# Head of a trunk kernel: the first key rows on ScalarE's DMA queue, the norm's sums four steps sooner, and three groups of edges that fix what follows what

## Chip, core and metric

The kernel runs on one core of one Trainium2 chip. The metric is the device time of one execution in microseconds (us). The kernel before takes 1174.61 us, the median of three runs (1174.42 to 1174.98). Profiles come from the hardware profiler, one execution each; times in a trace count from the start of its span.

## What is computed

One layer of a decoder trunk for 256 tokens of width 2048, in float32. The parts that this case touches:

```python
h = rms_norm(x, attn_norm[i])
z = h @ w_in[0]                                 # 2048 x 4384
zs = token_shift(z[..., POOL_WIDTH:], mu_shift) # z + (z_prev - z) * mu
...
w = -softplus(-(w0 + tanh(zw) @ w_up)) - 0.5
a = sigmoid(a0 + za @ a_up)
g = sigmoid(zg) @ g_up
```

z's columns are cut into a pool part, receptance (zr), key (zk), value (zv), each 1024 wide, and 288 columns of low-rank gates: 64 for zw, 64 for za, 160 for zg. Behind this come the pooling mixer, the RWKV scan with its norm, the output product, the feed-forward part with squared ReLU, a gated embedding and a last norm. All that is left as it is.

## The kernel before

Each weight panel (256 rows of the product, 512 columns, held as 128 partitions x 1024) is loaded as raw and split into a high part wh (ScalarE, two ACTIVATE of 512 columns, L168) and a low part wl (VectorE, one subtraction, L169). A product of tokens with such a panel is eight matmuls with wh (the activations' high part hTh at L244, low part hTl at L245) and then four with wl (L241), 512 columns each. raw, wh and wl have three buffers each, and a panel's load waits for the low part of the panel three before it.

The normed input is not made first: x is used with the norm's weight alone, and the factor 1/rms of each token (rs1) is put on the products as they leave the accumulators. So the squares' sums are needed only when the first product is copied out.

The head (L405 and on) runs two products side by side on the tensor engine (TensorE, PE in the profile): the 288 gate columns (wag_prod, in tiles of one or two rows of 128, banks wag_b) and the first key half (zk0, banks zk_b), whose generator gives its matmuls in steps. A step of a panel's first half is two matmuls, one of its second half a single one; a panel has eight steps. steps(n) gives n of them. ready(8) issues eight matmuls of ones ahead of the first operands. squares(q) squares a quarter of x on ScalarE and folds it on VectorE into the tile sqx; four matmuls with one column of ones then sum sqx over the partitions into sbank (L444). head_norm takes the root and the reciprocal. wag_out copies the gate banks out with rs1 as the scale (wagS), transposes them on TensorE (wagT, L467 and L468), and makes zf from them by shift_evac (an ACTIVATE, L338, and a VectorE operation that adds the token before, L339), with tanh on the first part and sigmoid on the rest. Behind that, z_zk0 finishes the key product, copies it out (zk0s, L491) and transposes it (zkT, L501).

What sets the order: TensorE's program order is the order of the code. VectorE's and ScalarE's is the code's only until early.close(), which stands behind wag_out. Calls under tc.high_priority are put forward by the scheduler, and tc.issue_after(ins) keeps an instruction of the same engine behind ins. The table behind does this for the ScalarE splits: behind["zk0_7"] = ins holds the split of panel 7 of zk0 (the eighth) behind ins. All loads of the head go through SP's queue in program order, except the parameters par_sb (ScalarE's queue, L83). GpSimd (POOL) makes constants early, then X (L715) and the four bands wband (L130 to L132), which VectorE finishes (L133 to L135); X lies in the memory of sqx's tiles and so waits for the matmuls that read them.

Of the kernel before, what the change touches and what calls it, by code (L numbers as in the profile page):

```python
# [16 lines left out]
T = 256  # L17
D = 2048
# [22 lines left out]
def trunk(  # L41
# [104 lines left out]

    deep = []

    def load_raw(src, n, name):
        own = False  # L150
        if deep:
            deep.append(name)
            own = len(deep) > 5 and len(deep) % 6 < 3
        if own:
            raw = fp.tile([128, 1024], F32, tag="raw2", bufs=3, name=f"raw_{name}")
        else:
            raw = wp.tile([128, 1024], F32, tag="raw", name=f"raw_{name}")
        nc.sync.dma_start(raw[:, 0:n], src)
        return raw

    def split_w(raw, name, after=None):

        wh = wp.tile([128, 1024], F32R, tag="wh", name=f"wh_{name}")
        wl = wp.tile([128, 1024], F32R, tag="wl", name=f"wl_{name}")
        with tc.high_priority(20000):
            for a in range(2):
                with tc.issue_after(after.ins) if after is not None else ExitStack():
                    nc.scalar.activation(wh[:, a * 512 : (a + 1) * 512], raw[:, a * 512 : (a + 1) * 512], AF.Copy)  # L168
            nc.vector.tensor_tensor(wl, raw, wh.bitcast(F32), op=ALU.subtract)  # L169
# [49 lines left out]

    behind = {}  # L220

    def gemm_toks(src, acts, name, consume, kps=None, hooks=()):

        banks = [mm_bank(f"{name}_b{i}") for i in range(2)]
        kps = list(range(src.shape[0])) if kps is None else kps
        hooks = dict(hooks)
        for i, kp in enumerate(kps):
            if kp in hooks:
                hooks[kp]()
            raw = load_raw(src[kp].rearrange("p a n -> p (a n)"), 1024, f"{name}_{kp}")  # L230
            halves = split_w(raw, f"{name}_{kp}", behind.get(f"{name}_{kp}"))
            for part in range(2):
                for a in range(2):
                    k = kp * 2 + a
                    a_ = acts(k)
                    ah, al = a_ if isinstance(a_, tuple) else (a_[:, 0, :], a_[:, 1, :])
                    for tt in range(2):
                        ts_ = slice(tt * 128, (tt + 1) * 128)
                        if part:
                            last = i == len(kps) - 1 and a == 1  # L240
                            nc.tensor.matmul(banks[tt], ah[:, ts_], halves[a][1], start=False, stop=last)  # L241
                            yield 0.23
                        else:
                            nc.tensor.matmul(banks[tt], ah[:, ts_], halves[a][0], start=i + a == 0, stop=False)  # L244
                            nc.tensor.matmul(banks[tt], al[:, ts_], halves[a][0], start=False, stop=False)  # L245
                            yield 0.45
        consume(banks)
# [105 lines left out]
    def load_xT(k0, n):  # L353
        nc.sync.dma_start(xq[k0 // 8][:, k0 // 4 % 2, k0 % 4 : k0 % 4 + n], xT[:, k0 : k0 + n, :])
# [46 lines left out]
    def ready(n):  # L401
        for _ in range(n):
            nc.tensor.matmul(rbank[:, 0:128], ones, ones, start=True, stop=True)

    def head():  # L405
        load_xT(0, 1)
        load_wag("tE", 0, 1)
        load_xT(1, 1)
        load_wag("tF", 1, 1)
        ready(8)  # L410
        wag_prod(0, 1)
        wag_prod(1, 1)
        steps(8)
        load_xT(2, 2)
        load_wag("zr", 2, 2)
        load_xT(4, 4)
        load_wag("zv", 4, 2)
        wag_prod(2, 2)
        wag_prod(4, 2)
        steps(8)  # L420
        sums.append(squares(0))
        load_wag("BK", 6, 2)
        load_xT(8, 4)
        load_wag("BKt", 8, 2)
# [12 lines left out]
        wag_prod(14, 2)
        steps(10)
        sums.append(squares(3))
        steps(3)  # L440
        derived()
        for tt in range(2):
            for i, q in enumerate((1, 3)):
                nc.tensor.matmul(  # L444
                    sbank[:, tt : tt + 1], sums[q][:, 0, tt * 128 : (tt + 1) * 128], ones[:, 0:1],
                    start=i == 0 and tt == 0, stop=i == 1, skip_group_check=True,
                )
        steps(1)

    rs1 = const.tile([128, 2], F32, tag="rs", bufs=2, name="rs_n1")  # L450

    def head_norm():
        nc.scalar.activation(rs1, sbank[:, 0:2], AF.Sqrt, bias=eps_n, scale=1.0 / D)
        nc.vector.reciprocal(rs1, rs1)

    zf = mixc.tile([128, 3, T], F32, name="zf")
    zwa, zg, zg2 = zf[:, 0], zf[:, 1], zf[0:64, 2]

    def wag_out():
        wagS = rp.tile([128, 576], F32, tag="SC", bufs=2, name="wagS")  # L460
        for tt in range(2):
            nc.scalar.activation(wagS[:, tt * 288 : (tt + 1) * 288], wag_banks[tt][:, 0:288], AF.Copy, scale=rs1[:, tt : tt + 1])
        tb, tb2 = rw_bank("wagT"), rw_bank("wagT2")
        for tt in range(2):
            c0 = tt * 288
            for i in range(2):
                nc.tensor.transpose(tb[:, i * T + tt * 128 : i * T + (tt + 1) * 128], wagS[:, c0 + i * 128 : c0 + (i + 1) * 128], ident)  # L467
            nc.tensor.transpose(tb2[0:32, tt * 128 : (tt + 1) * 128], wagS[:, c0 + 256 : c0 + 288], ident)  # L468
        mw = PARAM_COLS["mu_wag"]
        for i, (nm, src, pn) in enumerate((("zwa", tb[:, 0:T], 128), ("zg", tb[:, T : 2 * T], 128), ("zg2", tb2[0:32, 0:T], 32))):  # L470
            dst = zf[0:pn, i, :]
            shift_evac(dst, src, col("mu_wag", i)[0:pn], omu[0:pn, mw - m0 + i : mw - m0 + i + 1])
            if i == 0:
                nc.scalar.activation(dst[0:64], dst[0:64], AF.Tanh)
            else:
                nc.scalar.activation(dst, dst, AF.Sigmoid)
        nc.scalar.activation(zf[32:64, 2, :], zf[0:32, 2, :], AF.Copy)


    def z_product(i, tag, mu_name, gi, stage="a0"):  # L480

        box = []

        def consume(banks):
            if stage == "a0":
                zt = a8(0, f"{tag}{gi}s")[:, 0:1024].rearrange("p (a n) -> p a n", a=2)
            else:
                zt = rp.tile([128, 2, 512], F32, tag=stage, name=f"{tag}{gi}s")
            with tc.high_priority(30000):
                for tt in range(2):  # L490
                    nc.scalar.activation(zt[:, tt], banks[tt], AF.Copy, scale=rs1[:, tt : tt + 1])  # L491
            box.append(zt)

        def turn():
            zt = box.pop()
            dst = e4(tag)
            banks = [rw_bank(f"{tag}T{i}") for i in range(2)]
            for p in range(4):
                for tt in range(2):
                    o = p % 2 * T + tt * 128  # L500
                    nc.tensor.transpose(banks[p // 2][:, o : o + 128], zt[:, tt, p * 128 : (p + 1) * 128], ident)  # L501
            for p in range(4):
                c = PARAM_COLS[mu_name] - m0 + 4 * gi + p
                with tc.high_priority(30000):
                    shift_evac(dst[:, p, :], banks[p // 2][:, p % 2 * T : (p % 2 + 1) * T], col(mu_name, 4 * gi + p), omu[:, c : c + 1])
            return dst

        gen = queued(gemm_toks(w_in[i + gi], hT, f"{tag}{gi}", consume))

        def finished(us=1.70):  # L510
            finish(gen)
            fill(us)
            return turn()

        return finished
# [1052 lines left out]
```

## Time and profile before

| | |
|---|---|
| median of three runs | 1174.61 us |
| the profiled execution | 1175.37 us |
| its span | 1173.40 us |
| busy: TensorE, VectorE, ScalarE, GpSimd | 1160.2, 877.7, 713.5, 57.1 us |
| TensorE's clock as granted, mean | 0.999 |

The span is what the profiler saw of the core; the execution's time has 1.97 us more around it. In a timeline a row holds a run of like instructions: start, length of the run, engine, line, operation, output and inputs, shape, count, and in brackets the engine's idle time before with what ended it. Matmuls overlap, so the time of one in a stream is the distance of two starts, not its length.

### The profile page before, as it was taken

How to read it: one execution, taken by the hardware profiler on the slowest of the kernel's cores; microseconds unless marked ns; L12 is line 12 of the kernel's file. 1: busy time of each engine (PE TensorE's matmuls, PEld its weight loads, DVE VectorE, ACT ScalarE, POOL GpSimd, SP SyncE). 2: the span in 40 equal slices, each digit the busy share in tenths (PEclk: the TensorE clock that was granted, in tenths of full speed). 3: DMA queues.
4: the chain of work that ended last, by engine and by line, in shares of the span. 5: the costliest groups of instructions: out<-in, count | busy, mean ns of one | idle time of the engine just before them, and what ended most of it. 6: DMA issues, size and time to landing. Idle time of an engine off the chain costs nothing.

```text
span 1173.4 us, 17398 instructions
## 1 busy us (share of the span) xinstructions
PE 1160.2 (99%) x6407; PEld 972.1 (83%) x6407; DVE 877.7 (75%) x1194; ACT 713.5 (61%) x1323; POOL 57.1 (5%) x133
## 2 busy tenths in 40 slices
PE   9999999999999999999999999999999999999997
PEld 8788777888888888888888888888888888888886
DVE  7686996964756666766998997676768988897543
ACT  8776849676544565555664664555556665677543
POOL 2100000000000000000110110000000110000000
PEclk9999999999999999999999999999999999999999
DMA  7454343354455555565786786555555886975511
GB/s 292 154 202 147 131 139 117 129 180 161 161 200 178 180 183 194 197 216 180 223 246 213 229 254 218 193 186 193 184 193 165 260 254 220 323 241 188 197 55 72
DMA packets 67253, 224.42 MB, mean 191 GB/s; under 512 B 7712, under 2 KB 8480, under 8 KB 66784
## 3 DMA queue, kind: packets, MB, share of 16 engines
q1 hardware_dynamic: 60240, 207.38, 51.5%
q0 software_dynamic: 6496, 15.21, 5.7%
q8 instruction: 50, 0.82, 0.3%
q10 hardware_dynamic: 432, 0.73, 0.2%
q14 instruction: 35, 0.29, 0.1%
HBM read 221.19 MB, written 2.10 MB: 190 GB/s over the span
## 4 chain that ended last, share of the span: by engine, by line
PE 96%; DVE 2%; DMA 1%; ACT 1%; issue 0%; POOL 0%; SPq 0%; DVEq 0%; POOLq 0%; ACTq 0%
PE u_w L1136 20%; PE u_w L1141 10%; PE d_b L1293 7%; PE d_b L1295 7%; PE d_b L1294 7%; PE d_w L1293 2%; PE d_w L1295 2%; PE d_w L1294 2%; PE gt_b L244 2%; PE gt_b L245 2%; PE gt_b L241 2%; PE zp_b L241 1%; PE zv_b L244 1%; PE zv_b L241 1%; PE zk_b L244 1%; PE zv_b L245 1%
## 5 line engine op out<-in xcount | busy, mean ns | idle before, releaser
L1136 PE MATMUL u_w<-h,wh_u 128*128 128x512 f32 x1024 | 321.8, 396 | 0.0
L168 ACT ACTIVATE wh_u<-raw_u 128x512 fp32r<-128x512 f32 x256 | 147.5, 624 | 162.8 <-issue 101.8
L169 DVE TENSOR_TENSOR wl_u<-raw_u,wh_u 128x1024 fp32r<-128x1024 f32 x128 | 156.7, 1224 | 104.8 <-ACT wh_u L168 103.3
L1141 PEld LDWEIGHTS u_w<-h,wl_u 128*128 128x128 f32 x1024 | 192.7, 188 | 45.1
L1141 PE MATMUL u_w<-h,wl_u 128*128 128x256 f32 x1024 | 201.2, 278 | 0.0
L1136 PEld LDWEIGHTS u_w<-h,wh_u 128*128 128x128 f32 x1024 | 156.1, 189 | 0.2
L169 DVE TENSOR_TENSOR wl_gt<-raw_gt,wh_gt 128x1024 fp32r<-128x1024 f32 x24 | 29.4, 1224 | 23.2 <-ACT wh_gt L168 23.1
L173 ACT ACTIVATE wad<-ring 128x512 fp32r<-128x512 f32 x29 | 18.2, 628 | 43.9 <-DVE ring L1344 43.9
L168 ACT ACTIVATE wh_gt<-raw_gt 128x512 fp32r<-128x512 f32 x48 | 27.9, 633 | 24.2 <-PE gt_b L245 17.0
L244 PE MATMUL gt_b<-wh_gt,h 128*128 128x512 f32 x96 | 37.4, 390 | 0.0
L245 PE MATMUL gt_b<-wh_gt,h 128*128 128x512 f32 x96 | 37.4, 390 | 0.0
L1346 DVE TENSOR_TENSOR raw_d<-raw_d,ring 128x1024 f32<-128x1024 f32 x29 | 35.5, 1223 | 0.7
L1263 POOL DMA_DIRECT2D ring<-in_w_ffn_down_dram x29 | 16.5, 568 | 362.0 <-DVE wad L174 361.3
L1264 POOL DMA_DIRECT2D ring<-in_w_ffn_down_dram x29 | 25.3, 874 | 105.5 <-DMA ring<-in_w_ffn_down_dram 105.5
L169 DVE TENSOR_TENSOR wl_o<-raw_o,wh_o 128x1024 fp32r<-128x1024 f32 x16 | 19.6, 1223 | 12.9 <-ACT wh_o L168 11.4
L168 ACT ACTIVATE wh_o<-raw_o 128x512 fp32r<-128x512 f32 x32 | 18.4, 623 | 16.3 <-issue 8.5
L168 ACT ACTIVATE wh_zp<-raw_zp 128x512 fp32r<-128x512 f32 x32 | 18.6, 623 | 15.8 <-PE zp_b L245 7.2
L169 DVE TENSOR_TENSOR wl_zk<-raw_zk,wh_zk 128x1024 fp32r<-128x1024 f32 x16 | 19.4, 1222 | 10.2 <-ACT wh_zk L168 10.2
L244 PE MATMUL zv_b<-wh_zv,hTh 128*128 128x512 f32 x64 | 26.0, 406 | 0.0
L241 PE MATMUL gt_b<-wl_gt,h 128*128 128x512 f32 x96 | 25.8, 389 | 0.0
L244 PE MATMUL zp_b<-wh_zp,hTh 128*128 128x512 f32 x64 | 25.7, 401 | 0.0
L168 ACT ACTIVATE wh_zk<-raw_zk 128x512 fp32r<-128x512 f32 x32 | 18.4, 622 | 11.9 <-DMA raw_zk<-in_w_in_dram 5.7
(927 smaller groups left out, 3014.8 us busy)
## 6 DMA issues: line engine op xcount, KB each, us to landing
raw_u<-in_w_ffn_up_dram SPq DMA_DIRECT2D x128, 512.0 KB, 4.3
raw_d<-in_w_ffn_down_dram SPq DMA_DIRECT2D x99, 512.0 KB, 4.7
ring<-in_w_ffn_down_dram POOLq DMA_DIRECT2D x58, 256.0 KB, 4.6
raw_gt<-in_w_ple_gate_dram SPq DMA_DIRECT2D x24, 512.0 KB, 4.1
raw_zk<-in_w_in_dram SPq DMA_DIRECT2D x16, 512.0 KB, 3.8
raw_zr<-in_w_in_dram SPq DMA_DIRECT2D x16, 512.0 KB, 3.2
raw_zv<-in_w_in_dram SPq DMA_DIRECT2D x16, 512.0 KB, 3.3
raw_zp<-in_w_in_dram SPq DMA_DIRECT2D x16, 512.0 KB, 3.3
```

Of the source, the lines that this page charges most:

```text
L168: nc.scalar.activation(wh[:, a * 512 : (a + 1) * 512], raw[:, a * 512 : (a + 1) * 512], AF.Copy)
L169: nc.vector.tensor_tensor(wl, raw, wh.bitcast(F32), op=ALU.subtract)
L241: nc.tensor.matmul(banks[tt], ah[:, ts_], halves[a][1], start=False, stop=last)
L244: nc.tensor.matmul(banks[tt], ah[:, ts_], halves[a][0], start=i + a == 0, stop=False)
L245: nc.tensor.matmul(banks[tt], al[:, ts_], halves[a][0], start=False, stop=False)
L1136: nc.tensor.matmul(bank[:, ct, :].rearrange("p (s t) -> p s t", s=2), wh[:, cs[ct]], hl, start=k == 0, stop=False, skip_group_check=True,)
L1141: nc.tensor.matmul(bank[:, ct, 0:T], wl[:, cs[ct]], hl[:, 0, :], start=False, stop=k == 15, skip_group_check=True)
L1264: nc.gpsimd.dma_start(slot(n), w_down[pair, hf * 16 + kp, 0, :, 1, :], accum_op=ALU.add)
L1293: nc.tensor.matmul(banks[n], ah, wh, start=first, stop=False)
L1294: nc.tensor.matmul(banks[n], ah, wl, start=False, stop=False)
L1295: nc.tensor.matmul(banks[n], al, wh, start=False, stop=last)
L1346: nc.vector.tensor_tensor(t43, t43, t2.unsqueeze(1).to_broadcast([128, 2, 512]), op=ALU.subtract)
```

## The change

Six edits, all in the first 50 us.

1. The first half (one row of 128) of zk0's first panel is loaded on ScalarE's queue right behind the parameters, into a raw tile taken ahead of all others; SP loads the second half where it loaded the whole. Both halves are split one by one (split_rows).
2. Tile 1's loads are issued when zk0's generator starts, and two of its steps stand between tile 0 and tile 1 of the gate product; six follow.
3. After the last gate tile nine steps run instead of ten, then squares(3) and the sums' matmuls; the other five stand behind the wagS copies, ahead of wagT. Before, ten stood there, three more ahead of the sums and one behind them: fourteen both times.
4. Root, reciprocal and wagS copies get priority; the split of zk0's eighth panel (zk0_7) is held behind the second wagS copy.
5. tanh on the first part comes first, then the second part's shift, then a one-element sigmoid into warm, which brings its table load; the sigmoids themselves and the third part are held behind the key's copy-out zk0s.
6. The split of panel zr0_2 is held behind the same copy.

The core of the diff:

```diff
+    first_raw = wp.tile([128, 1024], F32, tag="raw", name="raw_zk0_0")
+    nc.scalar.dma_start(first_raw[:, 0:512], w_in[4, 0, :, 0, :])
...
-    def load_raw(src, n, name):
+    def load_raw(src, n, name, between=None):
...
+        if between is None:
+            nc.sync.dma_start(raw[:, 0:n], src)
+        else:
+            between()
+            nc.sync.dma_start(raw[:, 512:n], src[:, 512:n])
...
+    def split_rows(raw, name):
+
+        wh = wp.tile([128, 1024], F32R, tag="wh", name=f"wh_{name}")
+        wl = wp.tile([128, 1024], F32R, tag="wl", name=f"wl_{name}")
+        for a in range(2):
+            h, l, r = (t_[:, a * 512 : (a + 1) * 512] for t_ in (wh, wl, raw))
+            split_sb(h, l, r)
+            yield h, l
...
+    def second_rows():
+        load_xT(1, 1)
+        load_wag("tF", 1, 1)
+
     def head():
         load_xT(0, 1)
         load_wag("tE", 0, 1)
-        load_xT(1, 1)
-        load_wag("tF", 1, 1)
         ready(8)
         wag_prod(0, 1)
+        steps(2)
         wag_prod(1, 1)
-        steps(8)
+        steps(6)
...
-        steps(10)
+        steps(9)
         sums.append(squares(3))
-        steps(3)
         derived()
...
-        steps(1)
...
     def head_norm():
-        nc.scalar.activation(rs1, sbank[:, 0:2], AF.Sqrt, bias=eps_n, scale=1.0 / D)
-        nc.vector.reciprocal(rs1, rs1)
+        with tc.high_priority(30000):
+            nc.scalar.activation(rs1, sbank[:, 0:2], AF.Sqrt, bias=eps_n, scale=1.0 / D)
+            nc.vector.reciprocal(rs1, rs1)
...
+        behind["zk0_7"] = scaled
+        steps(5)
...
+        with tc.high_priority(30000):
+            dst = shifted(0)
+            nc.scalar.activation(dst[0:64], dst[0:64], AF.Tanh)
+            dst = shifted(1)
+            nc.scalar.activation(warm, eps_n, AF.Sigmoid)
+
+        def rest(after):
+            with tc.high_priority(30000), tc.issue_after(after.ins):
                 nc.scalar.activation(dst, dst, AF.Sigmoid)
-        nc.scalar.activation(zf[32:64, 2, :], zf[0:32, 2, :], AF.Copy)
+                last = shifted(2)
+                nc.scalar.activation(last, last, AF.Sigmoid)
+            nc.scalar.activation(zf[32:64, 2, :], zf[0:32, 2, :], AF.Copy)
+
+        return rest
...
+                    copied = nc.scalar.activation(zt[:, tt], banks[tt], AF.Copy, scale=rs1[:, tt : tt + 1])
             box.append(zt)
+            if (tag, gi) == ("zk", 0):
+                behind["zr0_2"] = copied
+                low_rank(copied)
...
-    z_zk0 = z_product(4, "zk", "mu_k", 0)
+    z_zk0 = z_product(4, "zk", "mu_k", 0, between=second_rows)
...
-    wag_out()
+    low_rank = wag_out()
```

How the programs stand on three engines around the norm. Names: zk0_5 is the sixth panel of the key product, sqx1 and sqx3 the two folded squares, wagS the scaled gates.

TensorE before, from the last but two high-part matmuls of panel zk0_5 to the gates' transposes:

```order
L245 MATMUL zk0_b0_216<-wh_zk0_5_486,hTl1_159 128x512
L244 MATMUL zk0_b1_217<-wh_zk0_5_486,hTh1_157 128x512
L245 MATMUL zk0_b1_217<-wh_zk0_5_486,hTl1_159 128x512
L241 MATMUL zk0_b0_216<-wl_zk0_5_487,hTh1_157 128x512
L444 MATMUL sbank_173<-ones_90,sqx1_370 128x1
L444 MATMUL sbank_173<-ones_90,sqx3_495 128x1
L444 MATMUL sbank_173<-ones_90,sqx1_370 128x1
L444 MATMUL sbank_173<-ones_90,sqx3_495 128x1
L241 MATMUL zk0_b1_217<-wl_zk0_5_487,hTh1_157 128x512
L467 MATMUL wagT_518<-ident_85,wagS_515 128x128 x2
```

TensorE of the change, from the first matmuls of the same panel (sbank is written at L467 there):

```order
L265 MATMUL zk0_b0_203<-wh_zk0_5_488,hTh1_159 128x512
L266 MATMUL zk0_b0_203<-wh_zk0_5_488,hTl1_161 128x512
L467 MATMUL sbank_175<-ones_92,sqx1_372 128x1
L467 MATMUL sbank_175<-ones_92,sqx3_495 128x1
L467 MATMUL sbank_175<-ones_92,sqx1_372 128x1
L467 MATMUL sbank_175<-ones_92,sqx3_495 128x1
L265 MATMUL zk0_b1_204<-wh_zk0_5_488,hTh1_159 128x512
```

The four sums moved ahead of seven key matmuls; behind them come six matmuls with wh and two with wl, and then wagT, which keeps its place.

ScalarE before, from the split of the eighth key panel to the first half of zk0s:

```order
L168 ACTIVATE wh_zk0_7_560<-raw_zk0_7_558 128x512 x2
L168 ACTIVATE wh_zr0_0_584<-raw_zr0_0_582 128x512 x2
L453 ACTIVATE rs_n1_175<-sbank_173,eps_n_79 128x2
L462 ACTIVATE wagS_515<-wag_b0_169,rs_n1_175 128x288
L462 ACTIVATE wagS_515<-wag_b1_170,rs_n1_175 128x288
L338 ACTIVATE zf_176<-wagT_518,omu_154 128x256
L474 ACT_TABLE_LOAD
L474 ACTIVATE zf_176<-zf_176 64x256
L168 ACTIVATE wh_zr0_1_622<-raw_zr0_1_620 128x512 x2
L338 ACTIVATE zf_176<-wagT_518,omu_154 128x256
L168 ACTIVATE wh_zr0_2_684<-raw_zr0_2_682 128x512 x2
L491 ACTIVATE zk0s_577<-zk0_b0_216,rs_n1_175 128x512
```

ScalarE of the change, from the second wagS copy, which stands right behind the root and the first copy:

```order
L486 ACTIVATE wagS_509<-wag_b1_172,rs_n1_177 128x288
L174 ACTIVATE wh_zk0_7_558<-raw_zk0_7_556 128x512 x2
L174 ACTIVATE wh_zr0_0_587<-raw_zr0_0_585 128x512
L359 ACTIVATE zf_178<-wagT_520,omu_156 128x256
L174 ACTIVATE wh_zr0_0_587<-raw_zr0_0_585 128x512
L508 ACT_TABLE_LOAD
L508 ACTIVATE zf_178<-zf_178 64x256
L359 ACTIVATE zf_178<-wagT_520,omu_156 128x256
L510 ACT_TABLE_LOAD
L510 ACTIVATE warm_83<-eps_n_81 128x1
L174 ACTIVATE wh_zr0_1_625<-raw_zr0_1_623 128x512 x2
L533 ACTIVATE zk0s_575<-zk0_b0_203,rs_n1_177 128x512
```

Two splits moved from ahead of the root to behind wagS, the split of zr0_2 from ahead of zk0s to behind it, and a table load from behind zk0s to ahead of wh_zr0_1.

VectorE before, from the constant cen on:

```order
L145 SCALAR_TENSOR_TENSOR cen_101<-jsum_92,ident_85 128x128
L169 TENSOR_TENSOR wl_zk0_7_561<-raw_zk0_7_558,wh_zk0_7_560 128x1024
L454 RECIPROCAL rs_n1_175<-rs_n1_175 128x2
L133 TENSOR_TENSOR wband_153<-wband_153,ident_85 128x128
L134 TENSOR_TENSOR wband_153<-wband_153,edge_125 128x16
```

VectorE of the change, from the second operation on the third band:

```order
L136 TENSOR_TENSOR wband_155<-wband_155,edge_127 128x16
L135 TENSOR_TENSOR wband_155<-wband_155,ident_87 128x128
L175 TENSOR_TENSOR wl_zk0_7_559<-raw_zk0_7_556,wh_zk0_7_558 128x1024
L360 SCALAR_TENSOR_TENSOR zf_178<-wagT_520,par_sb_77,zf_178 128x255
L175 TENSOR_TENSOR wl_zr0_0_588<-raw_zr0_0_585,wh_zr0_0_587 128x1024
```

The low half of the eighth key panel moved from ahead of the reciprocal to behind the third band's first operation (the second row), and stands now ahead of zf's shift. The first half panel takes a place in the rotation of the DMA semaphores, so SP's load for tile 4's gate columns now waits for it to have landed.

More of the change, by code (lines that the diff above doesn't have):

```diff
@@ L156, in load_raw @@
         else:
-            raw = wp.tile([128, 1024], F32, tag="raw", name=f"raw_{name}")
-        nc.sync.dma_start(raw[:, 0:n], src)
+            raw = wp.tile([128, 1024], F32, tag="raw", name=f"raw_{name}") if between is None else first_raw
+        if between is None:
[3 more added lines that the diff above has]
+            nc.sync.dma_start(raw[:, 512:n], src[:, 512:n])
         return raw
@@ L220, in trunk, with gemm_toks @@
     behind = {}
-    def gemm_toks(src, acts, name, consume, kps=None, hooks=()):
+    def gemm_toks(src, acts, name, consume, kps=None, hooks=(), between=None):
         banks = [mm_bank(f"{name}_b{i}") for i in range(2)]
@@ L229, in gemm_toks @@
                 hooks[kp]()
-            raw = load_raw(src[kp].rearrange("p a n -> p (a n)"), 1024, f"{name}_{kp}")
-            halves = split_w(raw, f"{name}_{kp}", behind.get(f"{name}_{kp}"))
+            first = between if i == 0 else None
+            raw = load_raw(src[kp].rearrange("p a n -> p (a n)"), 1024, f"{name}_{kp}", first)
+            if first is None:
+                halves = split_w(raw, f"{name}_{kp}", behind.get(f"{name}_{kp}"))
+            else:
+                halves, rows = [], split_rows(raw, f"{name}_{kp}")
             for part in range(2):
@@ L235, in gemm_toks @@
                     a_ = acts(k)
+                    if first is not None and not part:
+                        halves.append(next(rows))
                     ah, al = a_ if isinstance(a_, tuple) else (a_[:, 0, :], a_[:, 1, :])
@@ L460, in wag_out @@
         wagS = rp.tile([128, 576], F32, tag="SC", bufs=2, name="wagS")
-        for tt in range(2):
-            nc.scalar.activation(wagS[:, tt * 288 : (tt + 1) * 288], wag_banks[tt][:, 0:288], AF.Copy, scale=rs1[:, tt : tt + 1])
+        with tc.high_priority(30000):
+            for tt in range(2):
+                scaled = nc.scalar.activation(
+                    wagS[:, tt * 288 : (tt + 1) * 288], wag_banks[tt][:, 0:288], AF.Copy, scale=rs1[:, tt : tt + 1]
+                )
+        behind["zk0_7"] = scaled
+        steps(5)
         tb, tb2 = rw_bank("wagT"), rw_bank("wagT2")
@@ L469, in wag_out, with shifted, z_product @@
         mw = PARAM_COLS["mu_wag"]
-        for i, (nm, src, pn) in enumerate((("zwa", tb[:, 0:T], 128), ("zg", tb[:, T : 2 * T], 128), ("zg2", tb2[0:32, 0:T], 32))):
+        parts = (("zwa", tb[:, 0:T], 128), ("zg", tb[:, T : 2 * T], 128), ("zg2", tb2[0:32, 0:T], 32))
+        def shifted(i):
+            nm, src, pn = parts[i]
             dst = zf[0:pn, i, :]
             shift_evac(dst, src, col("mu_wag", i)[0:pn], omu[0:pn, mw - m0 + i : mw - m0 + i + 1])
[L473 to L476, printed above, removed]
-        nc.scalar.activation(zf[32:64, 2, :], zf[0:32, 2, :], AF.Copy)
-    def z_product(i, tag, mu_name, gi, stage="a0"):
+            return dst
+        with tc.high_priority(30000):
+            dst = shifted(0)
[4 more added lines that the diff above has]
+            with tc.high_priority(30000), tc.issue_after(after.ins):
+                nc.scalar.activation(dst, dst, AF.Sigmoid)
+                last = shifted(2)
+                nc.scalar.activation(last, last, AF.Sigmoid)
+            nc.scalar.activation(zf[32:64, 2, :], zf[0:32, 2, :], AF.Copy)
+        return rest
+    def z_product(i, tag, mu_name, gi, stage="a0", between=None):
         box = []
@@ L490, in consume @@
                 for tt in range(2):
-                    nc.scalar.activation(zt[:, tt], banks[tt], AF.Copy, scale=rs1[:, tt : tt + 1])
+                    copied = nc.scalar.activation(zt[:, tt], banks[tt], AF.Copy, scale=rs1[:, tt : tt + 1])
             box.append(zt)
+            if (tag, gi) == ("zk", 0):
+                behind["zr0_2"] = copied
+                low_rank(copied)
         def turn():
@@ L506, in turn @@
             return dst
-        gen = queued(gemm_toks(w_in[i + gi], hT, f"{tag}{gi}", consume))
+        gen = queued(gemm_toks(w_in[i + gi], hT, f"{tag}{gi}", consume, between=between))
         def finished(us=1.70):
```

## Prediction

> **What bounds the kernel now.** First the page's line of busy times, then the view of TensorE's waits, then its timeline (columns there: start, length, engine, line, operation, output and inputs, count, and in brackets the idle time before and its releaser).
>
> ```profile
> PE 1160.2 (99%) x6407; PEld 972.1 (83%) x6407; DVE 877.7 (75%) x1194; ACT 713.5 (61%) x1323; POOL 57.1 (5%) x133
> ```
>
> ```profile
> PE wagT L467 <- POOL wband L132: 1.5, 1, 1.5
> ...
> PE bsum L526 <- DVE zr_t L339: 1.0, 1, 1.0
> PE zkT L501 <- ACT zk1s L491: 0.8, 2, 0.6
> PE zk_b L244 <- ACT wh_zk L168: 0.4, 1, 0.4
> ```
>
> TensorE (PE) is busy 99% of the span, so time is won only where it waits. The change reaches two of these waits: that of wagT and that of zk_b, both in the first 38 us. The other two lie behind it, at 128 and 159 us.
>
> **The head, first 11 us.** TensorE's timeline, then ScalarE's, then the busy shares of two stretches (the last two columns are the DMA engines' share and GB/s).
>
> ```profile
> 5.74 0.65 PE L394 MATMUL wag_b<-wagl,hTh 128*128 128x288 f32 x2
> 6.53 0.40 PE L396 MATMUL wag_b<-wagh,hTh 128*128 128x288 f32 x1
> 6.77 0.29 PE L397 MATMUL wag_b<-wagh,hTl 128*128 128x288 f32 x1
> 6.91 0.29 PE L396 MATMUL wag_b<-wagh,hTh 128*128 128x288 f32 x1
> ...
> 7.98 0.50 PE L244 MATMUL zk_b<-wh_zk,hTh 128*128 128x512 f32 x1 [0.37 <-ACT wh_zk L168]
> ...
> 10.84 0.30 PE L396 MATMUL wag_b<-wagh,hTh 128*128 128x288 f32 x1
> ...
> 12.43 0.30 PE L396 MATMUL wag_b<-wagh,hTh 128*128 128x288 f32 x1
> ```
>
> ```profile
> 3.85 0.43 ACT L382 ACTIVATE wagh<-wag 128x288 fp32r<-128x288 f32 x1
> 5.58 0.51 ACT L381 ACTIVATE hTh<-xq,par_sb 128x256 fp32r<-128x256 f32 x1 [1.30 <-DMA xq<-in_xT_dram]
> ...
> 7.30 1.15 ACT L168 ACTIVATE wh_zk<-raw_zk 128x512 fp32r<-128x512 f32 x2 [0.82 <-DMA raw_zk<-in_w_in_dram]
> ...
> 10.49 0.91 ACT L381 ACTIVATE hTh<-xq,par_sb 128x256 fp32r<-128x256 f32 x2 [0.67 <-DMA xq<-in_xT_dram]
> 11.31 0.67 ACT L382 ACTIVATE wagh<-wag 128x576 fp32r<-128x576 f32 x1
> ```
>
> ```profile
> 1.50:5.00 3.50, 3.50 (x17) 3.50 (x17) 1.92 (x5) 2.09 (x4) 2.77 (x34) 1.00 0.74 208
> 5.00:20.50 15.50, 14.98 (x87) 13.32 (x87) 11.93 (x20) 12.93 (x25) 3.12 (x11) 1.00 1.03 401
> ```
>
> Matmuls start every 0.24 us (288 columns) until 6.77 and every 0.13 to 0.14 from there; a 512-wide one then takes 0.23 (2.86 us from 7.98 to 10.84 for twelve). TensorE starts the last wag matmul of tile 0 at about 5.98 and could go on at 6.22; it waits for tile 1's operands until 6.53, and the first key panel starts only at 7.98, since ScalarE gets the panel at 7.30.
>
> The change puts four matmuls of the panel's first row between tile 0 and tile 1. From 6.22: the first at the slow rate (0.24 x 512/288 = 0.43), one across the turn (about 0.30), two at 0.23: 7.41. Tile 1's six at 0.133: 8.21. The eight others of the panel at 0.23: 10.03, against 10.84. TensorE **leads by 0.8** if the operands are there. Needed: the half panel landed by 5.56, so that a split of 0.61 (half of the row at 7.30, and its overlap) ends at 6.2. ScalarE is free from 4.28 (row at 3.85) to 5.58. It is asked for on ScalarE's queue behind the parameters alone, where SP's old request stood behind four others. This trace has no such transfer. Bounds: the whole panel was there at 7.30; the parameters had landed by the row at 3.85, since the ACTIVATE ahead of it reads them. I take 5.0, nearer to the parameters, because the engines stood at 0.74 until 5.0 and 0.26 of 3.5 us (0.91 us) was room, while 256 KB at 401 GB/s need 0.64. The issue falls into ScalarE's wait for the parameters, so I cost it at nothing; without that cover it costs its own length.
>
> The lead must also hold behind 11 us, where the engines run at 1.03 and set the pace: ScalarE's row at 10.49 waits for a transfer, its split ends at 11.98, TensorE uses it at 12.43. So a lead over 0.40 is paid by earlier arrivals. The bytes are the same; what moves ahead of 5.0 makes all behind it earlier, 0 to 0.64 us. I take 0.4, so the lead is held to 0.8; with a little lost, **0.75** (ends: 0.35 for no earlier arrival; 0.2 if the fast rate came at 8.0, with all four at 0.43; 1.0).
>
> [...]
>
> **The norm, 33 to 47 us.** Timelines of TensorE, ScalarE, VectorE (DVE) and GpSimd (POOL).
>
> ```profile
> 33.45 0.39 PE L244 MATMUL zk_b<-wh_zk,hTh 128*128 128x512 f32 x1
> ...
> 35.05 0.95 PE L444 MATMUL sbank<-ones,sqx 128*128 128x1 f32 x8
> 35.86 0.48 PE L241 MATMUL zk_b<-wl_zk,hTh 128*128 128x512 f32 x1
> 37.83 0.41 PE L467 MATMUL wagT<-ident,wagS 128*128 128x128 f32 x2 [1.49 <-POOL wband L132]
> ```
>
> ```profile
> 35.66 1.15 ACT L168 ACTIVATE wh_zr<-raw_zr 128x512 fp32r<-128x512 f32 x2 [0.51 <-DMA raw_zr<-in_w_in_dram]
> 36.71 0.24 ACT L453 ACTIVATE rs_n<-sbank,eps_n 128x2 f32<-128x2 f32 x1
> 37.19 0.89 ACT L462 ACTIVATE wagS<-wag_b,rs_n 128x288 f32<-128x288 f32 x2 [0.23 <-DVE rs_n L454]
> ...
> 40.93 0.42 ACT L474 ACTIVATE zf<-zf 64x256 f32<-64x256 f32 x1 [0.55 <-DVE zf L339]
> ...
> 42.30 0.46 ACT L338 ACTIVATE zf<-wagT,omu 128x256 f32<-128x256 f32 x1
> ...
> 44.81 1.25 ACT L491 ACTIVATE zk0s<-zk_b,rs_n 128x512 f32<-128x512 f32 x2
> 46.07 1.28 ACT L476 ACT_TABLE_LOAD   x1
> 47.36 0.42 ACT L476 ACTIVATE zf<-zf 128x256 f32<-128x256 f32 x1
> ```
>
> ```profile
> 32.61 0.43 DVE L363 TENSOR_TENSOR sqx<-sqx,sqx 128x256 f32<-128x256 f32 x1
> ...
> 39.82 0.29 DVE L133 TENSOR_TENSOR wband<-wband,ident 128x128 f32<-128x128 f32 x1 [0.38 <-POOL wband L132]
> ...
> 40.42 0.47 DVE L339 SCALAR_TENSOR_TENSOR zf<-wagT,par_sb,zf 128x255 f32<-128x255 f32 x1
> 40.82 1.21 DVE L169 TENSOR_TENSOR wl_zr<-raw_zr,wh_zr 128x1024 fp32r<-128x1024 f32 x1
> ```
>
> ```profile
> 35.89 0.53 POOL L715 MEMSET X<- 128x512 f32 x1 [27.40 <-PE sbank L444]
> ...
> 39.48 0.30 POOL L132 TENSOR_SCALAR_AFFINE_SELECT wband<-wband 128x144 f32<-128x144 f32 x1
> ```
>
> The view puts the wait of wagT down to POOL, but wagT reads ident and wagS, and ident is the first tile that POOL makes: it waits for wagS. Its chain: sbank ends at 36.00, ScalarE is held by wh_zr until 36.71, then root, reciprocal and wagS, whose first half is out 0.45 after 37.19. One matmul after 35.86 would end at 36.09; wagT starts at 37.83. **Lost: 1.74 us** from start to start.
>
> Now the sums stand where the row at 33.45 stood, 1.60 earlier, and the root stands ahead of the splits of panels 8 and zr 0. From sbank's start: 0.95 to its end, 0.05, then root to wagS's end as before (38.08 - 36.71 = 1.37): 2.37. TensorE needs 0.81 for the sums and eight matmuls at 0.23, 2.65, until wagT. **The wait is gone**, with 0.28 to spare. The sums read sqx, ready at 33.04, less the 0.4 of earlier arrivals; TensorE comes at 33.45 - 0.75 = 32.70. So nothing is left to wait for here, but little slack; each 0.1 of missing earlier arrival costs 0.1.
>
> Late next is **ScalarE's copy of zk0s**. On it TensorE's transposes of zk wait:
>
> ```profile
> 45.82 1.27 PE L501 MATMUL zkT<-ident,zk0s 128*128 128x128 f32 x8
> ```
>
> Ahead of zk0s now stand, each waiting for the one before: POOL's third band, on VectorE the band, the low half of panel 8 (held back with its split) and zf's shift, on ScalarE the tanh, the second zf, a table load moved up from behind zk0s, and wh_zr 1. From sbank's start: third band out at 39.78 - 35.05 = 4.73; 0.24 for the band; 1.15 low half; 0.45 shift; 0.36 tanh; 0.38 zf (each row less the overlap with the next); 1.28 load; 0.12 for a 128x1 ACTIVATE, half of the 128x2 one at 36.71; 1.05 wh_zr; 1.25 zk0s: 11.0. Started at 32.70 it ends at 43.7, against 46.06: 2.35 earlier. TensorE would be 1.74 + 0.75 = 2.49 earlier. The later one decides: about **2.3 us** gained. The edits' other moves (the sigmoids and zr panel 2 behind zk0s) come after this point, with raw panels three buffers ahead, and I cost them at nothing; without that cover, one split's 1.15 in front of zk's shifts.
>
> **Sum.** The profiled execution took 1175.37 us (span 1173.40 and 1.97 around it), 0.76 over the median of 1174.61. 1175.37 - 2.3 = 1173.07; the same gain from the median gives 1172.31: **1172.3**.
>
> **Rivals.**
>
> *Half panel late (slower).* ScalarE's half panel shares the engines and stands on ScalarE ahead of tile 1's hTh (row at 5.58). Landing at t, the panel ends at t + 4.2 (0.66 + four and eight matmuls, 2.74, and tile 1, 0.80): even with before at 6.6. With the norm's 1.57 (the zk0s chain's gain without a lead) the kernel is slower from t = 8.2. Served only with the transfer that the row at 10.49 waits for, 2.2 slower: 1176.8. For it: the engines' 1.03 from 5.0 on. Against it: the parameters' landing on this queue. Chance 0.06.
>
> *No earlier rows (the first edit does nothing).* t = 7.3 gives 0.7 lost in the head, 0.9 gained in all: 1173.7. Chance 0.08.
>
> *ScalarE late before zk0s.* The row at 40.93, idle for 0.55 behind a load, allows a load up to that much more than its length. Two loads now stand in the chain: 1.1 less gained, 1173.4. Against it, the load at 46.07 ends at 47.35 and the next ACTIVATE starts at 47.36. Chance 0.08. [...]
>
> *Absorbed later.* The waits at 128 and 159 us could grow by the lead: 1174.2 to 1174.6.
>
> ```profile
> 125.32 0.24 PE zk_b L245
> ...
> 125.56 2.18 ACT wh_zr L168 x4
> ```
>
> In the chain of waits that stretch starts from TensorE, so it should move as a whole. Chance 0.09. *Better:* ScalarE's lead also shortens those waits: 1171.5. Chance 0.07.
>
> **How the numbers follow.** 0.62 for the forecast, 1171.8 to 1172.8. What a measurement of this kernel can tell from no change is about 0.2%, 2.35 us: the line is 1172.26, through the middle of the forecast, 0.33 of it below. Faster 0.33 + 0.07 = 0.40; slower 0.06; the rest 0.54. The range, 1171.4 to 1174.2, leaves out most of absorbed, the slower case and little else.
>
> **What would show it.** Right: the first key matmuls at 6.2 to 6.3 on TensorE, tile 2's wag at about 10.0, sums at 32.7, no wait before wagT, zk0s on ScalarE from about 42.5, zkT at about 43.4, and the waits at 128 and 159 unchanged in length and 2.3 earlier. Wrong: a DMA wait at the split of the first half panel beyond 5.6; a wait of the sums for sqx; a longer idle at zkT; waits of bsum above 1.0.

## The result, and the profile after

| | before | after |
|---|---|---|
| median, 22 runs each | 1175.56 us | 1173.91 us |
| lowest to highest | 1174.42 to 1177.78 | 1173.12 to 1176.11 |
| ratio, 95% interval | | 0.9985 (0.9980 to 0.9991) |
| profiled execution, its span | 1175.37, 1173.40 | 1175.02, 1173.1 |

The change gains 1.7 us, 0.15%, under the 0.2% that the prediction took as measurable; 22 runs each tell it from zero. The forecast was 1172.3, from a median of before (1174.61) that 22 runs put 0.95 higher; of the 2.3 us forecast, 1.7 came. The time lies in the stated range (1171.4 to 1174.2) but above the narrower forecast (1171.8 to 1172.8), and that it lies in the range is partly luck: the norm's part came, and the lead of the head, forecast at 0.75, is worth nothing that the runs can tell from zero (*norm_only* below).

The runs of one kernel fall in two groups here, and the text needs them: the change has 19 of 33 runs (these 22 and the 11 of *again* below) at 1172.9 to 1174.0 and 14 at 1174.7 to 1176.6. They are called the lower and the upper group. The profiled execution is of the upper one.

Waits of TensorE after:

```profile
...
PE bsum L571 <- DVE zr_t L360: 0.9, 1, 0.9
PE zkT L546 <- ACT zk1s L533: 0.8, 2, 0.6
PE wag_b L417 <- ACT wagh L403: 0.7, 1, 0.7
PE zkT L546 <- ACT zk0s L533: 0.2, 1, 0.2
```

The wait of wagT (1.5) and that of the first key panel (0.4) are gone; new are 0.7 ahead of tile 0's gate matmuls and 0.2 at the transposes of zk0s. The head after, TensorE's timeline and then ScalarE's (lines with "q" are DMA requests of the engine's sequencer):

```profile
1.20 3.78 PE L424 MATMUL rbank<-ones 128*128 128x128 f32 x16 [1.20 <-DVE ones L100]
5.68 0.61 PE L417 MATMUL wag_b<-wagh,hTh 128*128 128x288 f32 x1 [0.70 <-ACT wagh L403]
...
7.29 0.63 PE L265 MATMUL zk_b<-wh_zk,hTh 128*128 128x512 f32 x1
7.71 0.63 PE L266 MATMUL zk_b<-wh_zk,hTl 128*128 128x512 f32 x1
...
10.40 0.40 PE L265 MATMUL zk_b<-wh_zk,hTh 128*128 128x512 f32 x1
10.64 0.39 PE L266 MATMUL zk_b<-wh_zk,hTl 128*128 128x512 f32 x1
...
12.26 0.29 PE L417 MATMUL wag_b<-wagh,hTh 128*128 128x288 f32 x1
...
34.90 0.95 PE L467 MATMUL sbank<-ones,sqx 128*128 128x1 f32 x8
...
37.63 0.38 PE L495 MATMUL wagT<-ident,wagS 128*128 128x128 f32 x2
```

```profile
1.26 0.45 ACTq L85 DMA_DIRECT2D raw_zk<-in_w_in_dram  x1
...
5.18 0.44 ACT L403 ACTIVATE wagh<-wag 128x288 fp32r<-128x288 f32 x1 [1.26 <-DMA wag<-in_w_wag_dram]
5.54 0.62 ACT L188 ACTIVATE wh_zk<-raw_zk 128x512 fp32r<-128x512 f32 x1
...
44.79 1.25 ACT L533 ACTIVATE zk0s<-zk_b,rs_n 128x512 f32<-128x512 f32 x2
```

The half panel is there early (its split starts at 5.54 without a wait), but tile 0's gate rows came at 5.18 where ScalarE had them at 3.85 before. TensorE has done its ready matmuls at 4.98 and idles 0.70. It then works at about half its rate: 512-wide matmuls start 0.42 apart at 7.29, 0.24 apart from 10.40. Before, the starts show the fast rate from 6.77. Tile 2's gate matmuls start at 12.26, 1.42 later than the 10.84 of before; forecast was 0.8 earlier.

From there the forecast holds. From the sums' start to wagT are 2.73 us (worked out as 2.65) with no wait, and zk0s ends 11.14 behind the sums' start (44.79 + 1.25 - 34.90; worked out as 11.0). The head's 1.42 lost and the norm's gain leave 0.20 at wagT in this execution.

### The profile page after: what moved, and what is told of

It is laid out like the page before. It is cut to its first block, busy times and chain, and to the rows that moved or that the text cites. A ratio compares the mean times of both kernels' runs of the same rounds, so it can differ in the third digit from the quotient of the medians.

```text
span 1173.1 us, 17401 instructions
## 1 busy us (share of the span) xinstructions
PE 1160.6 (99%) x6407; PEld 972.9 (83%) x6407; DVE 878.2 (75%) x1195; ACT 714.1 (61%) x1324; POOL 58.9 (5%) x133
## 4 chain that ended last, share of the span: by engine, by line
PE 96%; DVE 2%; ACT 1%; issue 0%; DMA 0%; POOL 0%; DVEq 0%; SPq 0%; POOLq 0%
PE u_w L1181 20%; PE u_w L1186 10%; PE d_b L1338 7%; PE d_b L1339 7%; PE d_b L1340 7%; PE d_w L1339 2%; PE d_w L1338 2%; PE d_w L1340 2%; PE gt_b L265 2%; PE gt_b L262 2%; PE gt_b L266 2%; PE zp_b L262 1%; PE zv_b L265 1%; PE zv_b L262 1%; PE zv_b L266 1%; PE o_b L262 1%
## 5 line engine op out<-in xcount | busy, mean ns | idle before, releaser
L265 PE MATMUL zk_b<-wh_zk,hTh 128*128 128x512 f32 x64 | 25.7, 401 | 0.0
L266 PE MATMUL zk_b<-wh_zk,hTl 128*128 128x512 f32 x64 | 25.5, 398 | 0.0
```

## The experiments

All are compared with the kernel before on the same chip, and each computes everything. The ratios are those on record, close to the ratios of the means. *again*, *norm_only*, *head_only* and *ready10* are of one session; *later* and *ready6* are of a second, *sp_half* and *ready10_tail* of a third, *ready10_unheld* of a fourth. One run of the kernel before, at 2981.19 us, is left out of all counts.

**again**: the change, once more.

> The changed kernel once more, for a second trace. Crowded-start theory (the half panel takes the DMA engines from tile 0's gate rows; TensorE idles 0.7 us behind the ready matmuls and its fast rate comes some 3.5 us later): the gate rows land again at about 5.2, and a run with a short time (1173.1 to 1174.0) differs from one with a long time (1174.7 to 1176.1) by an earlier turn to the fast rate, near 7 instead of 10.4, and by nothing else. Rival (the profiled run was an odd one; the half panel mostly costs nothing): in a short run the gate rows land near 3.9 and tile 2's gate matmuls start near 10.0.

Measured: 1173.67 us, median of 11 (1172.88 to 1176.58); ratio 0.9991 (0.9982 to 0.9999). The profiled execution took 1172.88, so it shows the lower group. TensorE's timeline, then ScalarE's:

```profile
5.31 0.40 PE L417 MATMUL wag_b<-wagh,hTh 128*128 128x288 f32 x1 [0.48 <-ACT wagh L403]
5.55 0.30 PE L418 MATMUL wag_b<-wagh,hTl 128*128 128x288 f32 x1
5.68 0.30 PE L417 MATMUL wag_b<-wagh,hTh 128*128 128x288 f32 x1
...
6.22 0.39 PE L265 MATMUL zk_b<-wh_zk,hTh 128*128 128x512 f32 x1
...
10.04 0.30 PE L417 MATMUL wag_b<-wagh,hTh 128*128 128x288 f32 x1
...
32.67 0.95 PE L467 MATMUL sbank<-ones,sqx 128*128 128x1 f32 x8
35.40 0.38 PE L495 MATMUL wagT<-ident,wagS 128*128 128x128 f32 x2
43.37 0.27 PE L546 MATMUL zkT<-ident,zk0s 128*128 128x128 f32 x1
...
156.57 1.96 PE L571 MATMUL bsum<-ybuf,jsum 128*128 128x512 f32 x4 [0.87 <-DVE zr_t L360]
```

```profile
4.81 0.44 ACT L403 ACTIVATE wagh<-wag 128x288 fp32r<-128x288 f32 x1 [0.87 <-DMA wag<-in_w_wag_dram]
```

The gate rows are late here too (4.81), and TensorE idles 0.48; but the gate matmuls run 0.13 apart from 5.55, so the fast rate was there before the idle time ended (the expectation had it near 7). The starts on the forecast's list are met: first key matmul at 6.22, tile 2 at 10.04, sums at 32.67, zkT at 43.37. Some of that is luck: tile 0 starts 0.7 later than forecast and takes 0.9 where 1.6 was reckoned. The rival (rows near 3.9 in a short run) is refuted. The two executions of the change differ by 2.2 us at tile 2 and by 2.14 in time.

**norm_only**: first loads and steps of the head as before.

```diff
-    nc.scalar.dma_start(first_raw[:, 0:512], w_in[4, 0, :, 0, :])
...
         load_wag("tE", 0, 1)
+        load_xT(1, 1)
+        load_wag("tF", 1, 1)
         ready(8)
         wag_prod(0, 1)
-        steps(2)
         wag_prod(1, 1)
-        steps(6)
+        steps(8)
```

> The loads and the first steps of the head as before; everything from the sums on as in the change. Crowded-start theory: the whole gain is the norm's, 1.6 to 2.0 us below before, at least as fast as the change; sums at about 33.4, no wait before wagT. Rival (the head gains 0.75 as predicted and part of the norm's gain is lost later): 0.9 to 1.0 below before, slower than the change by 0.7.

Measured: 1174.04 (1173.20 to 1174.86), ratio 0.9987 (0.9978 to 0.9996). TensorE's timeline:

```profile
33.56 0.95 PE L462 MATMUL sbank<-ones,sqx 128*128 128x1 f32 x8
36.29 0.38 PE L490 MATMUL wagT<-ident,wagS 128*128 128x128 f32 x2
```

wagT starts 1.54 before the 37.83 of before, with no wait, and the lead stays: the span is 1171.8, 1.6 less than that of the first trace of before. Over the runs the gain is 1.1 in the median (1174.04 for 1175.15) and 1.4 in the mean (1174.07 for 1175.46), less than the 1.6 to 2.0 expected; the first trace of before had one of the longer waits of wagT (see *before2* to *before4*). With the head's part on top (*again*) the median is 0.37 lower (1173.67) and the mean 0.23 higher (1174.30): nothing that these runs can tell from zero.

**head_only**: the head as in the change; the norm, the sums and the edges as before.

```diff
-        steps(9)
+        steps(10)
         sums.append(squares(3))
+        steps(3)
...
-        behind["zk0_7"] = scaled
-        steps(5)
```

> Only the loads and first steps of the head as in the change; the norm, its sums and the edges as before. Crowded-start theory: no gain, between 0 and 1.5 us slower than before; gate rows at about 5.2; the wait of wagT stays at 1.5. Rival: 0.7 faster than before.

Measured: 1176.21 (1174.29 to 1176.96), ratio 1.0003 (0.9994 to 1.0011): no gain. ScalarE and TensorE:

```profile
5.44 0.44 ACT L403 ACTIVATE wagh<-wag 128x288 fp32r<-128x288 f32 x1 [1.53 <-DMA wag<-in_w_wag_dram]
```

```profile
5.94 0.61 PE L417 MATMUL wag_b<-wagh,hTh 128*128 128x288 f32 x1 [0.96 <-ACT wagh L403]
...
38.47 0.41 PE L491 MATMUL wagT<-ident,wagS 128*128 128x128 f32 x2 [0.85 <-POOL wband L132]
```

The wait of wagT fell to 0.85, against the expectation of 1.5: TensorE comes 1.3 later and wagS only 0.6 later. By the same means a lead of the head would go into this wait, so that without the norm's edits the head has little to win; that is argued, since no run has such a lead without them.

**ready10**: `ready(8)` becomes `ready(10)`.

> The change with ten ready matmuls in place of eight (two more, 0.47 us each as they stand in the trace, so the stream of them ends at 5.92 and not at 4.98, behind the arrival of the gate rows). Theory that the idle 0.70 us puts off the fast rate: the fast rate at 7.5 or sooner, tile 2's gate matmuls at 11.2 or sooner (12.26 in the change's profile), the time 0.8 to 1.4 us below the change's median and with less spread. Rival (the fast rate comes at an instant that has nothing to do with the idle time): the same spread as the change, and 0.24 us slower.

Measured: 1173.58 (1173.08 to 1174.28), ratio 0.9984 (0.9975 to 0.9993). TensorE:

```profile
1.20 4.63 PE L424 MATMUL rbank<-ones 128*128 128x128 f32 x20 [1.20 <-DVE ones L100]
5.48 0.59 PE L417 MATMUL wag_b<-wagh,hTh 128*128 128x288 f32 x1
...
6.55 0.43 PE L415 MATMUL wag_b<-wagl,hTh 128*128 128x288 f32 x2
6.82 0.39 PE L265 MATMUL zk_b<-wh_zk,hTh 128*128 128x512 f32 x1
```

Without idle time the fast rate is there at 6.55, and no run is above 1174.28, where the change has 14 of 33 at 1174.67 or above (the expectations say 13, a miscount). The median fell by 0.1 in place of 0.8: the median of the change lies in its lower group, so filling the gap shows in the spread and the mean (1173.59 for the 1174.30 of *again*). Against *norm_only*, of the same session, the head's edits with the gap filled are worth 0.46 in the median and 0.48 in the mean, though the two intervals overlap.

**ready6**: `ready(6)`.

> The change with six ready matmuls in place of eight: their stream ends at about 4.0, and TensorE idles 1.2 to 1.6 us before the gate rows come. If idle time puts off the fast rate: most runs in the slow group, median 1174.9 to 1175.6 (the change: 13 of its 33 runs at 1174.6 or above; with ten ready matmuls none of 11). Rival (the idle time has nothing to do with it): the change's median, 1173.7 to 1173.9, and its share of long runs.

Measured: 1174.10 (1172.91 to 1175.04), ratio 0.9986 (0.9977 to 0.9995). The median of 1174.9 did not come, nor the rival's 1173.7 to 1173.9. Five of its eleven runs are at 1174.6 or above, as are 14 of the change's 33, so a longer gap shows no larger share. The profiled one took 1172.91:

```profile
5.37 0.40 PE L417 MATMUL wag_b<-wagh,hTh 128*128 128x288 f32 x1 [1.24 <-ACT wagh L403]
5.61 0.29 PE L418 MATMUL wag_b<-wagh,hTl 128*128 128x288 f32 x1
```

1.24 us of idle time, and the fast rate all the same (starts 0.13 apart from 5.61). The packed traces also hold a record of the granted clock that starts with the turn to the fast rate. It has 4.22 for *ready6*, as its ready matmuls end (4.13), and 4.54 for *again*, whose gap starts at 4.82: in both the rate outlasted the gap, 1.24 and 0.48 us. The two traces that reach the gap without it (the change's 0.70 and *head_only*'s 0.96, both from 4.98) turned at 10.4 and 9.8.

**later**: the half panel's request behind the first ACTIVATE on ScalarE's queue.

> The change with the half panel's request moved on ScalarE's queue from ahead of the first table load to behind it (issue at about 3.1 in place of 1.3). Crowded-start theory: tile 0's gate rows land at 3.9 to 4.2 again, no idle time between the ready matmuls and tile 0, so no run with a late fast rate: all runs between 1172.9 and 1174.3, median 1173.4 or less. Rival (the half panel has to be asked for first to be of use): it lands behind 6.6, the first key matmuls wait, and the lead over norm_only goes: median 1174.0 or more.

Measured: 1173.65 (1173.26 to 1175.42), ratio 0.9988 (0.9979 to 0.9997). It didn't do what it was meant to:

```profile
1.33 0.38 ACTq L94 DMA_DIRECT2D raw_zk<-in_w_in_dram  x1
...
4.99 0.44 ACT L403 ACTIVATE wagh<-wag 128x288 fp32r<-128x288 f32 x1 [1.08 <-DMA wag<-in_w_wag_dram]
```

The sequencer issued the request at 1.33, while the table load still ran: 0.07 later than in the change. So it repeats the change, and one thing can be read from it:

```profile
5.48 0.40 PE L417 MATMUL wag_b<-wagh,hTh 128*128 128x288 f32 x1 [0.70 <-ACT wagh L403]
5.71 0.30 PE L418 MATMUL wag_b<-wagh,hTl 128*128 128x288 f32 x1
5.85 0.29 PE L417 MATMUL wag_b<-wagh,hTh 128*128 128x288 f32 x1
```

TensorE idles the same 0.70 as in the change's profile, and the fast rate is there: what differs is the turn, at 4.44, ahead of the gap.

**sp_half**: the half panel on SP's queue, behind tile 0's gate rows.

```diff
-    nc.scalar.dma_start(first_raw[:, 0:512], w_in[4, 0, :, 0, :])
...
         load_wag("tE", 0, 1)
+        nc.sync.dma_start(first_raw[:, 0:512], w_in[4, 0, :, 0, :])
```

> The change with the half panel asked for on SP's queue behind tile 0's gate rows, not on ScalarE's queue. Theory that the half panel takes tile 0's gate rows their place because it comes on another queue beside them: the gate rows land at 3.9 to 4.2 again, no idle time ahead of tile 0, no late fast rate: no run above 1174.4, median 1173.1 to 1173.6. Rival (any early half panel delays them, the queue doesn't matter): the gate rows at 4.8 or later, the median and the share of long runs as in the change (13 of 33 at 1174.6 or above).

Measured: 1174.16 (1173.69 to 1175.23), ratio 0.9990 (0.9981 to 0.9998). ScalarE, then TensorE:

```profile
3.90 0.43 ACT L402 ACTIVATE wagh<-wag 128x288 fp32r<-128x288 f32 x1
5.78 0.63 ACT L187 ACTIVATE wh_zk<-raw_zk 128x512 fp32r<-128x512 f32 x1 [1.45 <-DMA raw_zk<-in_w_in_dram]
```

```profile
6.46 0.50 PE L264 MATMUL zk_b<-wh_zk,hTh 128*128 128x512 f32 x1 [0.59 <-ACT wh_zk L187]
...
10.58 0.36 PE L416 MATMUL wag_b<-wagh,hTh 128*128 128x288 f32 x1
```

Behind them in one queue, the half panel leaves the gate rows alone (3.90): the rival that any early half panel delays them falls. The median is not better, though (1173.1 to 1173.6 was expected): the half panel comes at 5.78, and tile 2 starts at 10.58, a lead of 0.26. Five of its runs are above 1174.4, where none was expected. The profiled one (1174.44) is among them, and it turned at 5.08: not a late turn makes it long, but zkT, which starts 1.0 later than in *again*, and 0.4 of wait further on. No trace has both the gate rows near 3.9 and the half panel in time.

**before2, before3, before4**: the kernel before, three more traces.

> The kernel before once more, for a second trace; its runs fall in two groups as well (1174.2 to 1175.5 and 1176.4 to 1177.2). If a run falls in the upper group: theory that this is the head's fast rate too, the rate comes near 10 and tile 2's gate matmuls start at 12.4 or later; rival, something behind the head (the wait of wagT or the tail) is 1.5 us longer.

> The kernel before once more, for a third trace of it, in case the second falls in the lower group; the theories expect of it what they expect of before2.

> The kernel before once more, for a fourth trace, to find where its upper group (1176.4 to 1177.4, 26 of 75 runs) loses 1.7 us. Head theory: the fast rate comes later than 7.5. Norm theory: the wait of wagT is 3 us or more (1.2 to 1.9 in the three traces of the lower group).

Measured: 1174.47, 1175.28 and 1174.38, all of the lower group. The upper one (40 of 111 runs above 1175.9 in all) is in no trace, so both theories of it are untested and its cause stays open. The waits of wagT in the three, from the view of waits, one trace each:

```profile
PE wagT L467 <- POOL wband L131: 1.2, 1, 1.2
```

```profile
PE wagT L467 <- ACT wagS L462: 1.9, 1, 1.9
```

```profile
PE wagT L467 <- ACT wagS L462: 0.9, 1, 0.9
```

With the 1.5 of the first trace: 0.9 to 1.9 for the same program. The releaser named changes too. ScalarE's wagS in before3 and in before4:

```profile
37.57 0.89 ACT L462 ACTIVATE wagS<-wag_b,rs_n 128x288 f32<-128x288 f32 x2 [0.23 <-DVE rs_n L454]
```

```profile
36.60 0.89 ACT L462 ACTIVATE wagS<-wag_b,rs_n 128x288 f32<-128x288 f32 x2 [0.23 <-DVE rs_n L454]
```

wagT starts at 38.22 and 37.24 there. In all six traces that have the wait (these four, *head_only* and *ready10_unheld*) wagT starts 0.63 to 0.65 behind the start of wagS, whichever releaser is named. POOL's work behind the sums starts at 35.91 in before3 and 35.88 in before4, so it can't make the 0.98 between their wagT. wh_zr, which ScalarE works off ahead of the root, starts at 35.07 to 36.04 in the four traces and moves wagS. The times go with the wait in the main (1174.38, 1174.47, 1175.37, 1175.28 for 0.9, 1.2, 1.5, 1.9).

**ready10_unheld**: ready10 without the fourth edit.

```diff
-        with tc.high_priority(30000):
-            nc.scalar.activation(rs1, sbank[:, 0:2], AF.Sqrt, bias=eps_n, scale=1.0 / D)
-            nc.vector.reciprocal(rs1, rs1)
+        nc.scalar.activation(rs1, sbank[:, 0:2], AF.Sqrt, bias=eps_n, scale=1.0 / D)
+        nc.vector.reciprocal(rs1, rs1)
...
-        behind["zk0_7"] = scaled
```

> ready10 without the fourth edit: no priority for root, reciprocal and wagS, and the eighth key panel's split not held. In its order ScalarE has that split ahead of the root and the first receptance split (wh_zr 0, which waits for a load) ahead of the wagS copies; the sums stand where the change has them. Theory that the norm's gain comes from taking the root and wagS out from behind splits that wait for loads, and that the spread of the kernel before comes from there too (its wait of wagT was 0.92, 1.20, 1.49 and 1.86 us in four traces, always behind wh_zr 0): wagT waits 0.7 to 2.0 again, the median 0.7 to 1.8 above ready10's, at 1174.3 to 1175.4, with a spread over 1.5. Rival (the sums' place alone makes the gain): wagT waits less than 0.3, the median 1173.4 to 1173.9, a spread under 1.3 as ready10 has.

Measured: 1174.45 (1173.72 to 1175.21), ratio 0.9987 (0.9978 to 0.9996). ScalarE, then TensorE's waits:

```profile
34.37 0.24 ACT L475 ACTIVATE rs_n<-sbank,eps_n 128x2 f32<-128x2 f32 x1
35.79 1.15 ACT L174 ACTIVATE wh_zr<-raw_zr 128x512 fp32r<-128x512 f32 x2 [1.18 <-DVE rs_n L476]
36.84 0.87 ACT L484 ACTIVATE wagS<-wag_b,rs_n 128x288 f32<-128x288 f32 x2
```

```profile
PE wagT L490 <- POOL wband L132: 1.5, 1, 1.5
```

The sums stand where the change has them (33.05), but the wait of wagT is back at 1.5: wagT starts at 37.47, in *ready10* at 35.69, and the profiled executions took 1174.54 and 1173.26. The median is 0.87 above ready10's, of another session. The sums' place alone doesn't make the gain: ScalarE's order is needed. That order without the earlier sums was not run. The spread, 1.5, is at the edge of what was expected.

**ready10_tail**: ready10 with one store fewer.

```diff
-        nc.sync.dma_start(row[:, 640:1280], x_[:, 640:1280])
+        if tt:
+            nc.sync.dma_start(row[:, 640:1280], x_[:, 640:1280])
...
-        nc.sync.dma_start(row[:, 1280:2048], x_[:, 1280:2048])
+        c0 = 1280 if tt else 640
+        nc.sync.dma_start(row[:, c0:2048], x_[:, c0:2048])
```

> The change with ten ready matmuls and one store fewer at the end (the first token tile's two stores on SP's queue made one, so that the program has as many DMAs as before). Theory that the tail's 0.44 us (8.46 behind TensorE's last matmul in every trace with the half panel, 8.02 in every one without) comes from where SP's last wait stands in its list: one DMA more moves the last store from the last place of the list to the third, and seven waits of 0.06 us come behind it. By it the tail is 8.02 again and the median 0.4 below ready10's: 1173.1 to 1173.2. Rival (the tail's 0.44 belongs to the stores' transfers): the tail stays at 8.46 and the median at 1173.6.

Measured: 1173.07 (1172.95 to 1173.75), ratio 0.9982 (0.9973 to 0.9991). SP's waits at the end (L1609 and L1611 are the program's end), of ready10 and of this kernel:

```profile
SPq L1609 <- DMA out_dram<-x: 3.0, 1, 3.0
```

```profile
SPq L1611 <- DMA out_dram<-x: 2.6, 3, 1.2
```

At the end SP goes through a list of waits, one after the other. In the change's trace the one for the last store is the third: the store lands at 1171.74, SP goes on at 1171.76, and seven waits, 0.06 apart, come behind it, to 1172.18. In before's trace it is the last: landed at 1172.54, passed at 1172.56. From TensorE's last matmul to the span's end are 8.46 us in ready10 and 8.05 here, and the median is 0.5 lower. All eight traces with the half panel's DMA and all the stores have 8.44 to 8.47 there, the other six 8.02 to 8.05, so the 0.4 is shown; the rest of the 0.5 is between two sessions. It is the best version of the study and below both kernels' medians; its interval and the change's overlap.

## Why the prediction was right, and where it was not

- **The norm.** Right in mechanism: wagT's wait goes (1.5 to none) and comes back in ready10_unheld. That wagT waits for ScalarE's wagS, not for POOL, is shown by the 0.63 to 0.65 between the two in six traces. The size rests on one trace: its wait of 1.5 is one of 0.9, 1.2, 1.5 and 1.9, and norm_only gains 1.1 in the median and 1.4 in the mean, where the prediction reckoned 1.57 without a lead.
- **zk0s next.** Right: 11.14 for 11.0, and 0.2 of wait at zkT. The table load that was moved into that chain cost its length (42.34 to 43.62 in the change's profile, the next ACTIVATE at 43.64), so the rival of a late ScalarE didn't come.
- **The head's lead.** Right in size in one trace (0.80 in *again*) and wrong as a rule. The step that failed reads "I cost it at nothing": the issue was priced, the transfer's place in the engines was not. I took the engines' idle 0.26 before 5.0 as room, but the half panel's 256 KB run beside tile 0's 144 KB on a queue of their own, and the gate rows came 1.0 to 1.6 later (4.81 to 5.44 for 3.85). The engines' share from 1.5 to 5.0 rose only to 0.83 (the change) and 0.88 (*again*): a mean share below one didn't mean that another transfer costs nothing. With the two on two queues the gate rows came at 4.81 to 5.44 (five traces), with both on one at 3.90 (*sp_half*).
- **The turn to the fast rate.** The prediction took the 6.77 of one trace as fixed (the clock record has 6.2 there; behind a gap the first two starts are 0.23 to 0.24 apart at the fast rate too in *again*, *later*, *ready6* and *norm_only*, as at 5.31 and 5.55 in *again*). By the clock records the turn came at 4.1 to 4.5 in norm_only, ready6, later and *again*, at 5.1 to 6.8 in eight others, and at 10.4 and 9.8 in the change's profile and head_only. In that profile the turn at 10.4 in place of 6.8 or sooner is 3.6 us or more at about half rate (0.42 for 0.24 between starts), by my estimate about 1.8 lost; that every run of the upper group loses this is likely, but only one was traced. With the gap filled, in ready10, the upper group is gone (none of its 11 runs, nor of ready10_tail's 11). What sets the turn is not shown: *later* idles the same 0.70 as the change's profile and turned at 4.44, ahead of it, and no run isolates why.
- **Absorbed later.** This rival didn't come: from zkT to bsum are 113.20 in *again* and 113.26 in the change. Against the 113.62 of the first trace of before the lead seems to grow by 0.4, but the other three traces of before have 113.15 to 113.26.
- **The end.** Not seen: one DMA more costs 0.4 at the program's end.
- **Sum.** *again* leads the first trace of before by 0.80 at tile 2, 2.45 at zkT and 2.49 in time, close to the forecast. But its 1172.88 is the shortest of the change's 33 runs, and the 1175.37 lies above the middle of before's lower group. The medians of the two lower groups are 1173.45 and 1175.03, a gain of 1.6. The median of the change's upper group is 1175.07, so those runs have lost all of it again.

## What to carry to other kernels

A request that is made earlier can be paid by what the engines would have moved meanwhile (here the gate rows, at 4.81 to 5.44 for 3.85); ask which operand is needed first, and keep the two in one queue in that order (3.90 in *sp_half*). Take the short instruction that others wait for out from behind splits that wait for loads (the wait of wagT went from 1.5 to none); moving its inputs earlier brought little alone (1.5 again in *ready10_unheld*). Before a median is trusted at 0.1%, look whether the runs fall in groups, and take a trace of each.

## What was not expected of the hardware

- The granted clock of the windows view does not show TensorE's slow start: in the change's stretch from 5.7 to 10.4, where matmuls start 0.42 apart, it reads 1.00 (the column behind POOL's). The trace's clock record starts only with the turn, at 10.4.

```profile
5.70:10.40 4.70, 4.70 (x16) 4.31 (x17) 4.66 (x8) 3.97 (x9) 3.25 (x7) 1.00 1.00 385
```

- The fast rate, on record from 4.22, outlasted an idle time of 1.24 us (ready6).
- A DMA request that stands behind an ACTIVATE in ScalarE's program was issued before it began (later: 1.33, the ACTIVATE at 2.56).
- One DMA more at the start of the program, on ScalarE's queue or on SP's, moved its end by 0.4 us (8.44 to 8.47 behind TensorE's last matmul for 8.02 to 8.05).
